# A 4-byte-per-partition transfer from a constant tile to the output, issued ahead of the first load of an RMSNorm-SiLU kernel

## The chip, the cores and the metric

The kernel runs on one core of one Trainium2 chip. The metric is the device time of one launch in microseconds (us); lower is better. A profiled execution gives, beside its time, a span: from the first to the last instruction in the trace. Five engines work side by side, each with its own instruction queue: TensorE (PE), VectorE (DVE), ScalarE (ACT), GpSimd (POOL) and SyncE (SP). Data moves between the memory (HBM, called DRAM in the code) and the on-chip SBUF by 16 DMA engines that all queues share. Here ScalarE and SyncE issue transfers; each has a DMA queue of its own (q10 for ScalarE's transfers, q1 for SyncE's).

## The reference

```python
x: (8, 1024, 2048) float32; gamma: (2048,) float32; eps = 1e-5
rms = np.sqrt(np.mean(x ** 2, axis=-1, keepdims=True) + eps)
out = gamma * x / rms
return out * (1 / (1 + np.exp(-out)))
```

Each of the 8192 rows of 2048 values is divided by its root mean square, multiplied by gamma, and put through SiLU. All of x is read once and all of the output written once, 67.1 MB each.

## The kernel before

**Tiling.** The 8192 rows are cut into 16 blocks (`nblk`) of 512 rows. A block is one SBUF tile `xt` of 128 partitions x 8192 values: partition p holds J = 4 whole rows, which lie side by side in memory, so each partition's part is one run of 32 KB. `xb[b]` and `ob[b]` are the views of input and output for block b. A pool of BUFS = 6 such tiles is used in turn; the work is done in place, so a block's tile is loaded, computed on and stored from, and can be loaded again only when its store has landed.

**Work on one block.** `squares_scalar` (L65) sums the squares of one or two of the four rows on ScalarE, `squares_vector` (L73) those of the others on VectorE. `root` (L82) takes the root on ScalarE, `invert` (L87) its reciprocal on VectorE. `multiply` (L92) is four VectorE instructions, one for each row: x times the reciprocal times gamma. `silu` (L98) is two ScalarE instructions of two rows each, and `store` (L102) sends the block out. The last block is done otherwise: `multiply` by gamma alone (L152) while the root is computed, then Silu with the reciprocal as its scale (L154).

**Order.** The order is written out by hand: the body stands in `tc.manual_schedule()`, so each engine's instructions run in the order of the program, and semaphores for the dependences are added by the framework, for writes to the output in memory as well. The first thing is six loads, issued by ScalarE one behind the other (L54). Then VectorE fills `ones` and `eps_t`, ScalarE runs a Square on one element (L110), and SyncE issues the load of gamma into one partition (L111). TensorE spreads gamma over 128 partitions (L114) and VectorE copies it into `g` (L115). Then the loop over blocks starts. Loads 6 to 15 are issued by ScalarE from within `squares_scalar`, three blocks ahead, each behind a wait for the store that frees its tile. All 16 stores are issued by SyncE, in order, each when its block's Silu is done.

**Queues.** ScalarE's queue holds both compute and load issues: an issue that waits holds up the compute behind it. SyncE's queue holds gamma's load and the 16 stores. A transfer signals its landing on one of eight semaphores that are taken in rotation.

**Constant tiles.** The framework's start-up has GpSimd fill small constant tiles before the kernel's body begins, among them one of 128 x 1 float32 zeros (`const-float32-0.0`).

Of the kernel before, what the change touches and what calls it, by code (L numbers as in the profile page):

```python
# [1 line left out]

# [4 lines left out]

ACT = mybir.ActivationFunctionType
ALU = mybir.AluOpType


@with_exitstack
def kernel(
    ctx: ExitStack,
    tc: tile.TileContext,
    x: bass.AP,
    gamma: bass.AP,
    eps: bass.AP,
    out: bass.AP,
):  # L20

    nc = tc.nc
    P = nc.NUM_PARTITIONS
    f32 = mybir.dt.float32
    x2 = x.flatten_outer_dims()
    o2 = out.flatten_outer_dims()  # L30
    n, d = x2.shape
    J = 4
    BUFS = 6
    nblk = n // (P * J)
    xb = x2.rearrange("(b p j) d -> b p (j d)", p=P, j=J)
    ob = o2.rearrange("(b p j) d -> b p (j d)", p=P, j=J)

    singles = ctx.enter_context(tc.tile_pool(name="singles", bufs=1))
    pool = ctx.enter_context(tc.tile_pool(name="pool", bufs=BUFS))
    small = ctx.enter_context(tc.tile_pool(name="small", bufs=2))  # L40
    psum = ctx.enter_context(tc.tile_pool(name="psum", bufs=1, space=bass.MemoryType.PSUM))

    Q = 4
    w = d // Q
    g = singles.tile([P, d], f32)
    eps_t = singles.tile([P, 1], f32)
    ones = singles.tile([P, P], f32)
    junk_a = psum.tile([P, d], f32, name="junk_a")
    junk_v = psum.tile([P, d], f32, name="junk_v")
    blocks, sss, rmss, rstds = {}, {}, {}, {}  # L50

    def load(b):
        xt = pool.tile([P, J * d], f32, name="xt")
        nc.scalar.dma_start(out=xt, in_=xb[b])  # L54
        blocks[b] = xt

    def row(b, j):
        return blocks[b][:, j * d:(j + 1) * d]

    def squares_scalar(b, loads=()):  # L60


        sss[b] = small.tile([P, J], f32, name="ss")
        for j in range(share(b)):
            nc.scalar.activation(out=junk_a, in_=row(b, j), func=ACT.Square,  # L65
                                 accum_out=sss[b][:, j:j + 1])
            if j == 0:
                for s in loads:
                    load(s)

    def squares_vector(b):
        for j in range(share(b), J):
            nc.vector.tensor_tensor_reduce(  # L73
                out=junk_v, in0=row(b, j), in1=row(b, j), scale=1.0, scalar=0.0,
                op0=ALU.mult, op1=ALU.add, accum_out=sss[b][:, j:j + 1])

    def share(b):
        return 1 if 4 <= b <= 12 and b % 2 == 0 else 2

    def root(b):  # L80
        rms = small.tile([P, J], f32, name="rms")
        nc.scalar.activation(out=rms, in_=sss.pop(b), func=ACT.Sqrt, scale=1.0 / d, bias=eps_t)  # L82
        rmss[b] = rms

    def invert(b):
        rstd = small.tile([P, J], f32, name="rstd")
        nc.vector.reciprocal(out=rstd, in_=rmss.pop(b))  # L87
        rstds[b] = rstd

    def multiply(b):  # L90
        for j in range(J):
            nc.vector.scalar_tensor_tensor(out=row(b, j), in0=row(b, j), scalar=rstds[b][:, j:j + 1],  # L92
                                           in1=g, op0=ALU.mult, op1=ALU.mult)

    def silu(b):
        for h in range(0, J, 2):
            cols = slice(h * d, (h + 2) * d)
            nc.scalar.activation(out=blocks[b][:, cols], in_=blocks[b][:, cols], func=ACT.Silu)  # L98
        store(b)

    def store(b):
        nc.sync.dma_start(out=ob[b], in_=blocks[b])  # L102

    with tc.manual_schedule():

        for b in range(BUFS):
            load(b)
        nc.vector.memset(ones, 1.0)  # L108
        nc.vector.memset(eps_t, float(eps))
        nc.scalar.activation(out=junk_a[:, 0:1], in_=ones[:, 0:1], func=ACT.Square)  # L110
        nc.sync.dma_start(out=g[0:1, :], in_=bass.AP(tensor=gamma.tensor, offset=gamma.offset, ap=[[d, 1], [1, d]]))  # L111
        for c in range(Q):
            cols = slice(c * w, (c + 1) * w)
            nc.tensor.matmul(junk_v[:, cols], ones[0:1, :], g[0:1, cols], start=True, stop=True)  # L114
        nc.vector.tensor_copy(out=g, in_=junk_v)  # L115

        last = nblk - 1
        SOON = 3  # L120
        squares_scalar(0)
        squares_vector(0)
        root(0)
        invert(0)
        for b in range(last):
            loads = [b + 3] if BUFS <= b + 3 < nblk else []
            if b < SOON:
                multiply(b)
                squares_scalar(b + 1, loads)
                silu(b)  # L130
                squares_vector(b + 1)
                root(b + 1)
            elif b < last - 1:
                squares_scalar(b + 1, loads)
                squares_vector(b + 1)
                root(b + 1)
                multiply(b)
                silu(b)
            else:
                multiply(b)  # L140
                squares_scalar(b + 1)
                silu(b)
                squares_vector(b + 1)
                root(b + 1)
            if b + 1 < last:
                invert(b + 1)


        for j in range(J):
            if j == J // 2:  # L150
                invert(last)
            nc.vector.tensor_mul(out=row(last, j), in0=row(last, j), in1=g)  # L152
        for j in range(J):
            nc.scalar.activation(out=row(last, j), in_=row(last, j), func=ACT.Silu,  # L154
                                 scale=rstds[last][:, j:j + 1])
        store(last)


# [1 line left out]
_INS = ['x', 'gamma', 'eps']  # L160
_OUTS = [((8, 1024, 2048), 'float32')]

_NUMBERS = {'eps': 9.999999747378752e-06}


# [26 lines left out]
```

## Time and profile before

| What | Value |
|---|---|
| median of five runs | 316.89 us |
| five runs, lowest to highest | 316.72 to 317.34 us |
| the profiled execution's own time | 316.89 us |
| its span | 315.1 us |
| busy: DVE, ACT, PE | 235.3, 213.9, 7.2 us |
| HBM read, written | 67.12 MB, 67.11 MB |
| share of the 16 DMA engines: q10 (loads), q1 (gamma and stores) | 49.7%, 49.4% |
| DMA packets; of these under 512 B | 4612; 513 |
| issue to landing, median: a load, a store | 38.7 us, 29.6 us |
| shortest: a load, a store | 12.3 us, 13.4 us |
| first and last load issue | 0.7 us, 240.5 us |
| first and last store issue | 35.2 us, 300.9 us |

A load or a store is 4.19 MB in 128 runs of 32 KB, 8 of them for each DMA engine, and each DMA engine ends its part with a 4-byte write to the semaphore. Those writes are the packets under 512 B: 16 for each of 32 transfers and one for gamma's. In the start of the trace GpSimd fills the constants at 0.23 to 0.43 us, and the first issues on both queues stand at 0.72 us. ScalarE's first Square on a block begins at 13.10 us, when the first load has landed.

### The profile page before, as it was taken

To read this page: it belongs to the slowest core of one execution; us is meant where nothing else is said; L and a number is where in the kernel's file an instruction comes from. 1 tells how busy PE (TensorE), PEld (TensorE's weight loads), DVE (VectorE), ACT (ScalarE), POOL (GpSimd) and SP (SyncE) were. 2 spreads that over 40 slices of the span, in tenths; PEclk is the share of its full clock that TensorE was granted. 3 is DMA by queue.
4 is the path that set the end of the run, shared out by engine and by line. 5 is a ranking of instruction groups with operands and counts; after the bars stand their busy time and mean duration, and the time that the engine had idled before them with its cause. 6 is when DMAs were issued, how large, how long until landed. Compare 5 with 4: busy or idle time off the path is not lost.

```text
span 315.1 us, 437 instructions
## 1 busy us (share of the span) xinstructions
PE 7.2 (2%) x8; PEld 2.5 (1%) x8; DVE 235.3 (75%) x157; ACT 213.9 (68%) x136; POOL 0.2 (0%) x4
## 2 busy tenths in 40 slices
PE   6200000000000000000000000000000000000000
PEld 2000000000000000000000000000000000000000
DVE  0679597979995795957969489593996929999600
ACT  1349998972799268682687827877278768779910
POOL 0000000000000000000000000000000000000000
DMA  8999999999999999999999999999999999999996
GB/s 334 408 458 408 395 462 408 458 416 449 416 450 412 450 412 453 416 449 420 445 424 441 433 433 437 428 437 428 441 424 441 424 441 424 445 420 449 416 449 287
DMA packets 4612, 134.24 MB, mean 426 GB/s; under 512 B 513, under 2 KB 513, under 8 KB 513
## 3 DMA queue, kind: packets, MB, share of 16 engines
q10 hardware_dynamic: 2304, 67.11, 49.7%
q1 hardware_dynamic: 2306, 67.12, 49.4%
q14 instruction: 2, 0.02, 0.0%
HBM read 67.12 MB, written 67.11 MB: 426 GB/s over the span
## 4 chain that ended last, share of the span: by engine, by line
DMA 68%; DVE 14%; ACT 11%; issue 2%; ACTq 1%; DVEq 0%
DMA xt<-in_x_dram 68%; DVE xt L92 9%; DVE junk_v L73 5%; ACT xt L98 4%; ACT junk_a L65 3%; ACT xt L154 2%; ACT L82 1%; ACTq L187 1%; ACT L154 0%; ACT L98 0%; ACT rms L82 0%; DVE ss L73 0%; ACTq L54 0%; DVE rstd L87 0%; ACTq L82 0%
## 5 line engine op out<-in xcount | busy, mean ns | idle before, releaser
L92 DVE SCALAR_TENSOR_TENSOR xt<-xt,rstd,g 128x2048 f32<-128x2048 f32 x60 | 137.0, 2346 | 0.1
L98 ACT ACTIVATE xt<-xt 128x4096 f32<-128x4096 f32 x30 | 108.3, 3615 | 27.1 <-DVE xt L92 27.0
L73 DVE CUSTOM_DVE_ANT_0 junk_v<-xt 128x2048 f32<-128x2048 f32 x37 | 85.1, 2299 | 43.0 <-DMA xt<-in_x_dram 42.3
L65 ACT ACTIVATE junk_a<-xt 128x2048 f32<-128x2048 f32 x27 | 50.7, 1877 | 22.4 <-DMA xt<-in_x_dram 22.0
L82 ACT ACT_TABLE_LOAD x15 | 19.2, 1283 | 27.6 <-DVE ss L73 27.5
L98 ACT ACT_TABLE_LOAD x14 | 18.0, 1283 | 0.2
L87 DVE RECIPROCAL rstd<-rms 128x4 f32<-128x4 f32 x16 | 2.8, 173 | 8.3 <-ACT rms L82 8.3
L152 DVE TENSOR_TENSOR xt<-xt,g 128x2048 f32<-128x2048 f32 x4 | 8.9, 2279 | 0.0
L115 DVE COPY g<-junk_v 128x2048 f32<-128x2048 f32 x1 | 2.3, 2291 | 8.8 <-PE junk_v L114 8.8
L82 ACT ACTIVATE rms<-ss,eps_t 128x4 f32<-128x4 f32 x16 | 4.8, 297 | 5.7 <-DVE ss L73 5.5
L154 ACT ACTIVATE xt<-xt,rstd 128x2048 f32<-128x2048 f32 x4 | 7.7, 1990 | 0.0
L114 PE MATMUL junk_v<-g,ones 1*128 1x512 f32 x8 | 7.2, 1072 | 2.6 <-DMA g<-in_gamma_dram 2.6
L73 DVE DVE_READ_ACCUMULATOR2_ANT ss<- 128x1 f32 x37 | 5.2, 141 | 0.0
L65 ACT ACTIVATION_READ_ACCUMULATOR junk_a<-xt 128x1 f32 x27 | 5.0, 186 | 0.0
L110 ACT ACT_TABLE_LOAD x1 | 1.3, 1283 | 4.0 <-issue 4.0
L114 PEld LDWEIGHTS junk_v<-g,ones 1*128 1x128 f32 x8 | 2.5, 325 | 5.7 <-issue 5.7
L154 ACT ACT_TABLE_LOAD x1 | 1.3, 1283 | 0.0
L108 DVE MEMSET ones<- 128x128 f32 x1 | 0.2, 165 | 0.8 <-PEq L173 0.8
L110 ACT ACTIVATE junk_a<-ones 128x1 f32<-128x1 f32 x1 | 0.2, 174 | 0.0
L173 POOL MEMSET const-bfloat16-1.0<- 128x1 bf16 x1 | 0.1, 101 | 0.0
L173 POOL MEMSET const-uint8-127<- 128x1 uint8 x1 | 0.1, 101 | 0.0
L173 POOL MEMSET const-float32-0.0<- 128x1 f32 x1 | 0.1, 98 | 0.2 <-issue 0.2
(2 smaller groups left out, 0.2 us busy)
## 6 DMA issues: line engine op xcount, KB each, us to landing
xt<-in_x_dram ACTq DMA_DIRECT2D x16, 4096.0 KB, 38.7
out_dram<-xt SPq DMA_DIRECT2D x16, 4096.0 KB, 29.6
g<-in_gamma_dram SPq DMA_DIRECT2D x1, 8.0 KB
```

Of the source, the lines that this page charges most:

```text
L65: nc.scalar.activation(out=junk_a, in_=row(b, j), func=ACT.Square, accum_out=sss[b][:, j:j + 1])
L73: nc.vector.tensor_tensor_reduce(out=junk_v, in0=row(b, j), in1=row(b, j), scale=1.0, scalar=0.0, op0=ALU.mult, op1=ALU.add, accum_out=sss ...
L82: nc.scalar.activation(out=rms, in_=sss.pop(b), func=ACT.Sqrt, scale=1.0 / d, bias=eps_t)
L87: nc.vector.reciprocal(out=rstd, in_=rmss.pop(b))
L92: nc.vector.scalar_tensor_tensor(out=row(b, j), in0=row(b, j), scalar=rstds[b][:, j:j + 1], in1=g, op0=ALU.mult, op1=ALU.mult)
L98: nc.scalar.activation(out=blocks[b][:, cols], in_=blocks[b][:, cols], func=ACT.Silu)
L110: nc.scalar.activation(out=junk_a[:, 0:1], in_=ones[:, 0:1], func=ACT.Square)
L114: nc.tensor.matmul(junk_v[:, cols], ones[0:1, :], g[0:1, cols], start=True, stop=True)
L115: nc.vector.tensor_copy(out=g, in_=junk_v)
L152: nc.vector.tensor_mul(out=row(last, j), in0=row(last, j), in1=g)
L154: nc.scalar.activation(out=row(last, j), in_=row(last, j), func=ACT.Silu, scale=rstds[last][:, j:j + 1])
L187: with _tile.TileContext(nc) as tc:
```

## The change

ScalarE issues one more transfer, in front of the six loads: the 128 x 1 tile of zeros goes to the first element of each partition's run in block 0 of the output, 128 pieces of 4 bytes that lie 32 KB apart in memory. Store 0 writes the same places later, so the framework lets it wait until this transfer has landed; the output is the same. Nothing else is changed; the lines below move down by two.

```diff
     with tc.manual_schedule():
 
+        zero = nc.const_aps.tensor(0.0, [P, 1], f32)
+        nc.scalar.dma_start(out=ob[0][:, 0:1], in_=zero, allow_slow_non_contiguous=True)
         for b in range(BUFS):
             load(b)
         nc.vector.memset(ones, 1.0)
```

## The prediction

> **What bounds the kernel now.** I read the page's slices first, then the queues, the chain of waits, windows of the DMA rows at the start, at the first store and at the end, and last what the issuing queues wait for. The slices, from the page:
>
> ```profile
> DVE  0679597979995795957969489593996929999600
> ACT  1349998972799268682687827877278768779910
> DMA  8999999999999999999999999999999999999996
> GB/s 334 408 458 408 395 462 408 458 416 449 416 450 412 450 412 453 416 449 420 445 424 441 433 433 437 428 437 428 441 424 441 424 441 424 445 420 449 416 449 287
> ```
>
> No compute engine is full, but the 16 DMA engines are busy from the first slice to the last. The alternation of 408 and 458 is counting: pieces of 32 KB are booked whole where they start. In windows that hold whole rounds of pieces it is gone (columns: window, its length, the five engines, clock, DMA share, GB/s):
>
> ```profile
> 26.79:38.88 12.10, 0.00 (x0) 0.00 (x0) 8.80 (x7) 12.02 (x8) 0.00 (x0) 1.00 1.01 415
> 50.98:63.08 12.10, 0.00 (x0) 0.00 (x0) 10.48 (x6) 11.46 (x9) 0.00 (x0) 1.00 1.00 433
> ...
> 278.50:302.69 24.19, 0.00 (x0) 0.00 (x0) 17.90 (x11) 21.56 (x13) 0.00 (x0) 1.00 1.00 433
> 300.00:312.10 12.10, 0.00 (x0) 0.00 (x0) 0.00 (x0) 0.84 (x1) 0.00 (x0) 1.00 1.00 433
> ```
>
> The ceiling is 433 GB/s, 27.06 GB/s per engine, or 1.21 us for one 32 KB piece. All 134.22 MB at that rate take 310.0 us of the 315.1 us span. The last line matters: even after the last load, while the tail computes, the engines still work off earlier stores, so a delay anywhere in the DMA reaches the end whole. Only 5.1 us of the span is not transfer at full rate. Three views show where part of that lies. First the chain of waits, at its start:
>
> ```profile
> 0.66 0.06 issue
> 0.72 0.38 ACTq L54
> 1.11 0.03 issue
> 1.14 21.57 DMA xt<-in_x_dram
> ```
>
> ScalarE's first issue starts at 0.72 us and its second at 1.14, 0.42 later. Then the DMA rows of 1.5 to 3.1 us (the first load's first round of pieces) and of 37.2 to 38.7 us (the round in which the first store, issued at 35.23, joins):
>
> ```profile
> DMA packets 18, 0.53 MB, mean 333 GB/s; under 512 B 1, under 2 KB 1, under 8 KB 1
> q10 hardware_dynamic: 16, 0.52, 116.0%
> q1 hardware_dynamic: 2, 0.01, 2.1%
> ```
>
> ```profile
> DMA packets 16, 0.52 MB, mean 350 GB/s; under 512 B 0, under 2 KB 0, under 8 KB 0
> q10 hardware_dynamic: 16, 0.52, 118.9%
> ```
>
> The percentage is packet time over 16 engines and the window. One load piece per engine took 1.160 x 1.6 = 1.86 us at the start and 1.189 x 1.5 = 1.78 us where the first store joins, against 1.21 in steady state: two one-time stalls of 0.65 and 0.57 us. The second agrees with the dip to 415 GB/s above: (1 - 415/433) x 12.1 = 0.50 us. No other 24.19 us window up to 302.69 us is under 432 GB/s.
>
> **The change part by part.** *The added issue (L107).* It stands on ScalarE's queue in front of all six first loads. Nothing shows an issue of such small pieces; I price it as a load's, which has 128 pieces too: the first issue delays the second by 0.42 us, and the six together took 3.21 us, 0.54 each. I take 0.42 (the same place in the queue) and keep 0.54 as the upper end. Loads 1 to 5 move too, but only the first matters: the six are 25.2 MB, 58 us at 433 GB/s, queued within 4 us. Behind them on ScalarE stand the table load at 3.96 us and the one-element Square; ScalarE then sits idle 7.67 us until the first load lands (13.10), which hides them. Gamma goes on SyncE's queue and is not moved in time; it shares the engines, and its copy ends at 12.10, 7.7 us before its first use by L92 at 19.82.
>
> *The 128 pieces of 4 bytes.* Each of 16 engines gets 8 and a completion write. The trace has no 4-byte data piece. Below, the nearest row is the completion write, 4 bytes too, in the last window (312.7 to 315.1 us):
>
> ```profile
> DMA packets 16, 0.00 MB, mean 0 GB/s; under 512 B 16, under 2 KB 16, under 8 KB 16
> q1 hardware_dynamic: 16, 0.00, 0.4%
> ```
>
> That is 0.004 x 2.4 us x 16 / 16 = about 0.01 us each, so 9 of them are 0.09 us per engine. Above, the smallest data piece is gamma's 8 KB: q1's 2.1% of 16 x 1.6 us is 0.54 us, less the 0.01 of its completion, against 8192 B / 27.06 GB/s = 0.30 by size: 0.23 us of overhead. Eight such are 1.84 us, and with one completion 1.85. I take the lower price, since size is what the piece shares with it, but add one stall: twice in this trace the first use of something in the DMA (first load; first write to the output) cost 0.57 to 0.65 us, and the pieces are now the first of their queue and the first write. Their work is then 0.65 + 0.09 = 0.74 us, of which the 0.42 us until the first load's pieces arrive is already counted: 0.32 more.
>
> By the Trainium skill ("DMA: Bandwidth & Descriptors", Specifications) a transfer under 512 B makes the engine read, modify and write, and its section on latency and other measured facts gives about 0.8 us as the least round trip to HBM. That speaks against the change: were the round trip blocking once, the 0.74 would be an estimate of 0.89 by that page, and the total 0.15 higher; were it blocking eight times, 6.4 us. No row here shows a 4-byte write to the output, but the completion writes behind 4 MB stores show no pause: the store-only window above stays at 433 GB/s across one.
>
> *The wait of the first store.* It is on SyncE's queue, in front of all 16 stores, for the tiny transfer's landing. That store is issued at 35.23 us, when its Silu ends. The tiny transfer, issued at 0.72, would have to take over 34 us to be felt; the whole first load took 12.3. Cost zero, hidden by load 0's compute. If the cover were gone, every us late would delay store 0, the reuse of its buffer by load 6, and all stores behind it. The semaphores of later transfers shift by one place in their rotation of eight; each transfer waits for the same predecessors as before, so nothing else is added.
>
> *What may be given back.* The 0.57 us stall at the first store may be the price of the first write to the output, which the tiny transfer now pays in advance, or the price of a second queue joining a running one (SyncE's), which it can't pay, as it runs on ScalarE's. Bounds 0 and -0.57; I take 0, because the stall stands on the load's pieces while a new queue starts, and the tiny transfer leaves that as it is.
>
> Sum: 0.42 + 0.32 + 0 + 0 = +0.74 us on a profiled execution of 316.89 us (span 315.1 and 1.8 around it), which is also the median of the five runs: 317.63. Own range: low 0.42 + 0.09 - 0.09 hidden in the 0.42 = +0.42 (no stall), high 0.54 + 0.65 + 1.85 - 0.42 = +2.62.
>
> **The rivals.** *A, the first store's stall is taken over.* The tiny write pays for the first write of each engine and the dip near 37 us goes: 0.74 - 0.57 = +0.17, 317.06. For it: the stall occurs once, at the first write to the output, though stores and loads take turns for 240 us after it. Against: gamma's queue start, the other joining, fell into the first load's stall and can't tell the two apart.
>
> *B, faster.* The place is the first round of both queues. The tiny pieces pay every first-use cost while load 0 is still being issued: load 0's first round drops from 1.86 to 1.21 (-0.65), the first store's too (-0.57), and in front stand only the issue and pieces, 0.42 + 0.09 = 0.51: -0.71, 316.18. It decides once over 0.51 us of the two stalls, 1.22 together, is gone; with one gone it is A or nothing. For it: both stalls look alike. Against: the load's may simply be the time until the first bytes of x come back, which a write elsewhere doesn't shorten.
>
> *C, heavy pieces.* At gamma's overhead of 0.23 us each: 0.42 + (0.65 + 1.85 - 0.42) = +2.50, 319.4; half of that overhead gives +1.58, 318.5. For it: nothing in the trace shows a small data piece cheaper than 0.54 us. Against: that is one row, taken inside the start stall.
>
> **How the numbers follow.** The forecast (front delay paid, nothing given back) has 0.46, A 0.16, B 0.20, C 0.18. The time is the forecast's, 317.6. About 0.2% (0.63 us; limits 316.26 and 317.52) is what a measurement of this kernel can tell from no change, its five runs spreading over 0.62 us. The forecast sits 0.11 us above that limit, and 0.06 of its 0.46 I put below it; with A the middle has 0.22. Faster is B, 0.20; slower is 0.40 + 0.18 = 0.58. The range goes down to 316.1, which takes in B's own value, and up to 318.9, which leaves out the upper half of C: about 0.1 is left out on each side. The forecast alone runs from 317.3 (+0.42) to 318.3 (half of C's surcharge).
>
> **What would show it.** Some 144 more packets, all under 512 B. ScalarE's first load issue 0.42 to 0.54 us later, the first load's landing later by 0.7; the dip to 415 GB/s still there near 38 us, and 433 everywhere else. If the dip is gone, A or B; if load 0's first round takes 1.21 us, B; if the tiny packets' queue time exceeds 1 us per engine, C. The forecast is wrong if the last store's issue (300.87) moves by less than 0.4 or more than 1.5 us, or if any window past 40 us leaves 433 GB/s: that would be a mechanism I have not seen.

## The result and the profile after

| | before | after |
|---|---|---|
| median | 316.91 us (49 runs) | 317.45 us (29 runs) |
| ratio | | 1.0017, 95% interval 1.0012 to 1.0022 |
| profiled execution: span | 315.1 us | 315.6 us |

The change makes the kernel 0.54 us slower, 0.38 to 0.70 by the interval of the ratio. That is within the 0.2% (0.63 us) which the prediction had called no change, and inside its range; the forecast was 317.6. Of all timed runs in this document one, 329.51 us of the kernel that writes 4 KB in advance, was in a slow state and is left out of its comparison.

First the page of the kernel after: the added packets and the issues.

```profile
DMA packets 4756, 134.24 MB, mean 425 GB/s; under 512 B 657, under 2 KB 657, under 8 KB 657
...
q10 hardware_dynamic: 2448, 67.11, 49.7%
q1 hardware_dynamic: 2306, 67.12, 49.3%
...
out_dram<-const-float32-0.0 ACTq DMA_DIRECT2D x1, 0.5 KB, 1.9
```

There are 144 more packets, all under 512 B and all on ScalarE's queue: 128 pieces and 16 completion writes. The tiny transfer lands 1.9 us after its issue, 33 us before the first store needs it. The chain of waits of the kernel after, at its start:

```profile
0.72 0.39 ACTq L107
1.11 0.03 issue
1.14 0.46 ACTq L54
```

The tiny issue now stands at 0.72 us and load 0's at 1.14: the 0.42 us of the prediction. What the DMA engines do meanwhile is in the DMA row of 1.5 to 3.5 us, in 40 slots of 0.05 us (busy tenths above, GB/s below). Before:

```profile
DMA  0060999999990990090000000000000000000009
GB/s 0 0 164 0 1311 1311 655 1311 655 1311 655 655 0 655 1311 0 0 655 0 0 0 0 0 0 0 0 0 0 0 0 0 0 0 0 0 0 0 0 0 655
```

After:

```profile
DMA  0094420000000199990909090000900090000000
GB/s 0 0 166 4 3 1 0 0 0 0 0 0 0 1 1966 655 1966 1966 0 655 0 655 0 655 0 0 0 0 1311 0 0 0 655 0 0 0 0 0 0 0
```

A packet is booked in the slot where it starts; 164 GB/s is gamma's 8 KB, 655 one piece of 32 KB. Before, load 0's first pieces start in the slot at 1.70 us. After, the 4-byte pieces (4, 3 and 1 GB/s) stand at 1.60 to 1.80, then nothing starts until load 0's pieces in the slot at 2.20, 0.50 us later than before, but for nine 4-byte packets at 2.15, right behind the completion write of gamma (one engine's share). So load 0 does not wait for the pieces to be worked off: for the last 0.4 us the other engines stand empty, until the next transfer reaches them. From the issue of load 0 to its first piece it is 1.06 us (1.14 to 2.20), against 0.98 before (0.72 to 1.70): of the 0.50, 0.42 are the issue. How long a 4-byte piece takes is in the DMA row of 1.2 to 2.2 us of the kernel after:

```profile
DMA packets 145, 0.01 MB, mean 9 GB/s; under 512 B 144, under 2 KB 144, under 8 KB 144
q10 hardware_dynamic: 143, 0.00, 7.7%
```

0.077 x 16 x 1.0 us / 143 is 8.6 ns. Load 0's first round is as slow as it was: in the window of 1.5 to 3.5 us its 16 pieces and the tiny ones stand as

```profile
q10 hardware_dynamic: 160, 0.52, 95.0%
```

which is 1.90 us per engine, or 1.82 us without nine packets of 8.6 ns each, against 1.86 before. The last of the 16 pieces of this round starts in the slot at 3.10 us, before at 2.35, and the first load lands when the last engine is through. ScalarE's first Square begins 0.73 us later than before (13.10):

```profile
13.83 1.88 ACT L65 ACTIVATE junk_a<-xt 128x2048 f32<-128x2048 f32 x1 [7.94 <-DMA xt<-in_x_dram]
```

The first store's issue goes with it (35.98 instead of 35.23). The prediction gave 0.7 for that landing; the end moved by less.

The stall where the first store joins is still there (windows of whole rounds, columns as in the prediction):

```profile
27.20:39.30 12.10, 0.00 (x0) 0.00 (x0) 8.78 (x8) 12.04 (x9) 0.00 (x0) 1.00 1.00 417
37.10:61.29 24.19, 0.00 (x0) 0.00 (x0) 21.89 (x14) 22.39 (x17) 0.00 (x0) 1.00 1.00 419
61.29:85.48 24.19, 0.00 (x0) 0.00 (x0) 22.27 (x17) 13.29 (x10) 0.00 (x0) 1.00 1.00 433
```

417 and 419 GB/s around the first store, as 415 and 419 before, and 433 behind it. At the other end, the completion writes of the last store: before, 9 of the 16 DMA engines write theirs between 313.0 and 313.3 us; after, 10 of them between 313.6 and 313.9. The delay of the start has gone through 310 us of saturated DMA and comes out at the end.

### The profile page after: what moved, and what is told of

The parts are those of the page before. It is cut to its first block, busy times and chain, and to the rows that moved or that the text cites. A ratio compares the mean times of both kernels' runs of the same rounds, so it can differ in the third digit from the quotient of the medians.

```text
span 315.6 us, 438 instructions
## 1 busy us (share of the span) xinstructions
PE 7.2 (2%) x8; PEld 2.5 (1%) x8; DVE 235.3 (75%) x157; ACT 213.7 (68%) x136; POOL 0.2 (0%) x4
## 4 chain that ended last, share of the span: by engine, by line
DMA 68%; DVE 14%; ACT 11%; issue 2%; ACTq 1%; DVEq 0%
DMA xt<-in_x_dram 68%; DVE xt L92 9%; DVE junk_v L73 5%; ACT xt L98 4%; ACT junk_a L65 3%; ACT xt L156 2%; ACT L82 1%; ACTq L189 1%; ACT L156 0%; ACT L98 0%; ACT rms L82 0%; DVE ss L73 0%; ACTq L54 0%; ACTq L107 0%; DVE rstd L87 0%
```

## The experiments

The theory after the first result: the change costs the place of one transfer in front of load 0, that is, the 0.5 us by which load 0's pieces start later, and its size, its direction and the wait of the first store cost nothing. The rivals: the 4-byte pieces or the write to HBM cost it (a cold start, slow pieces); or the first store's wait does. Each kernel was timed against the kernel before on the same chip. The diffs of the first seven stand against the changed kernel, the others against the kernel before.

**Behind load 0 instead of in front of it.**

```diff
         for b in range(BUFS):
             load(b)
+            if b == 0:
+                nc.scalar.dma_start(out=ob[0][:, 0:1], in_=zero, allow_slow_non_contiguous=True)
```

(and the line in front of the loop is gone)

> The tiny transfer is issued by ScalarE behind load 0 instead of in front of it; its pieces and the first store's wait stay. If the 0.54 us that the change costs is the place in front of load 0 (0.42 us of issue, 0.6 us until load 0's pieces start), it falls to the pieces alone, 9 x 0.01 = 0.09 us: 317.0. If it is the pieces (a cold start, a slow 4-byte write) or the store's wait, it stays near 317.45, wherever the transfer stands.

317.20 against 316.94 us, ratio 1.0007 (0.9998 to 1.0016): not told apart from no change, though the interval (up to 0.51 us) also overlaps the change's. Load 0's pieces start in the slot at 1.70 us again. By itself this run leans to the place as the cost; the next one, which is clearer, decides. (The 1.6 us that this expectation and the next name as the start of the pieces is gamma's slot; load 0's is 1.70.)

**Issued by SyncE.**

```diff
-        nc.scalar.dma_start(out=ob[0][:, 0:1], in_=zero, allow_slow_non_contiguous=True)
+        nc.sync.dma_start(out=ob[0][:, 0:1], in_=zero, allow_slow_non_contiguous=True)
```

> The tiny transfer is issued by SyncE in front of gamma, so ScalarE's first load issue is back at 0.72 us. If the cost is ScalarE's issue slot: 317.0, load 0's pieces at 1.6 us as before. If both queues' transfers are prepared one after another by something shared, load 0 starts up to 0.5 us later: 317.2 to 317.4. If the stall of 0.57 us at the first store (37 us) is the price of the first write on SyncE's queue, the dip to 415 GB/s goes, and the time falls to 316.4 to 316.9; if it is the price of two busy queues meeting, the dip stays.

317.02 against 316.94 us, ratio 0.9999 (0.9989 to 1.0009): no cost that shows. The same 128 pieces to the same place, with the same wait of the first store, are free when they don't stand in ScalarE's queue. The DMA row of this kernel, 1.5 to 3.5 us:

```profile
DMA  0055399909990009000900000000000000000000
GB/s 0 0 4 4 2 656 1966 2621 0 1311 655 1966 0 0 0 655 0 0 0 655 0 0 0 0 0 0 0 0 0 0 0 0 0 0 0 0 0 0 0 0
```

Here the pieces of both queues follow each other with no empty slot: the pieces at 1.60 to 1.75, load 0's from 1.75. So a transfer on the other queue does not hold load 0 up, and one on the same queue does. What was held up is gamma, now second on SyncE's queue: TensorE's first matmul, which waits for it, began at 7.15 us instead of 2.61, and the first store was issued at 36.16 instead of 35.23. The time did not follow that, so a later first store alone is not what the change costs. The stall at the first store did not go (one round of 16 load pieces between 38.4 and 39.9 us takes 115.1% of 1.5 us, 1.73 us each, and 33.0 to 45.1 us runs at 412 GB/s), so a first small write on SyncE's queue doesn't pay for it.

**Two in front.**

```diff
         nc.scalar.dma_start(out=ob[0][:, 0:1], in_=zero, allow_slow_non_contiguous=True)
+        nc.scalar.dma_start(out=ob[0][:, 1:2], in_=zero, allow_slow_non_contiguous=True)
```

> Two such transfers in front of load 0, on the first and the second column. If each costs its issue slot: 0.54 more, or 0.46 to 0.6, so 317.9 to 318.1, and load 0's issue at about 1.6 us. If the cost is paid once (a cold start of the queue or of the first write): near 317.55.

318.27 against 316.94 us, ratio 1.0039 (1.0026 to 1.0052): +1.33 us by the medians, more than twice the change. Load 0's issue is at 1.62 us as expected, but its pieces start only in the slot at 2.90, 1.20 later than before. By the medians the time follows the pieces (1.20) rather than the issue (0.90), but its interval, 0.82 to 1.65 us, takes in both. From the issue of load 0 to its first piece it is now 1.28 us, where it was 0.98 with none and 1.06 with one such transfer in front. That the queue prepares its transfers one behind the other, and more slowly than ScalarE issues them, would fit this; no row shows the preparing itself.

**One piece instead of 128.**

```diff
-        nc.scalar.dma_start(out=ob[0][:, 0:1], in_=zero, allow_slow_non_contiguous=True)
+        nc.scalar.dma_start(out=ob[0][0:1, 0:1], in_=zero[0:1, :], allow_slow_non_contiguous=True)
```

> The tiny transfer has one piece of 4 bytes (partition 0 alone) instead of 128, still in front of load 0. If the cost is that of issuing a transfer whatever its pieces: 317.4. If it goes by pieces (their preparation or their work on the engines): 1/128 of it, so 316.9 to 317.1, with load 0's issue less than 0.2 us later.

317.61 against 316.94 us, ratio 1.0019 (1.0011 to 1.0028): the cost of the change, with one 4-byte piece. It is the transfer, not its pieces. ScalarE is even held longer (its next issue stands at 1.28 us instead of 1.14), and load 0's pieces start in the slot at 2.25, 0.97 us behind the issue as in the kernel before. Here the issue alone makes the delay: it is 0.56 us later, the pieces 0.55.

**64 times the pieces.**

```diff
-        zero = nc.const_aps.tensor(0.0, [P, 1], f32)
-        nc.scalar.dma_start(out=ob[0][:, 0:1], in_=zero, allow_slow_non_contiguous=True)
+        zero = nc.const_aps.tensor(0.0, [P, 64], f32)
+        nc.scalar.dma_start(out=ob[0][:, 0:128:2], in_=zero, allow_slow_non_contiguous=True)
```

> Same place in front of load 0, but 64 pieces of 4 bytes per partition (every second element of the first 128), 8192 in all, 512 per DMA engine. One look at the price of a piece. If a piece costs its row in the trace, 0.01 us: 512 x 0.01 = 5 us of engine time ahead of load 0, 322. If the pieces are written at gamma's overhead of 0.23 us each: about 118 us more. If the preparation of the transfer goes by its pieces, ScalarE's next issue comes later than 0.42 us as well.

365.57 against 316.88 us, ratio 1.153 (1.152 to 1.155): +48.7 us for 512 pieces per DMA engine, 95 ns each if all of it is put down to them, eleven times their price in the change and under half of gamma's 0.23. Two stretches of this kernel's DMA rows show both prices, first 1.0 to 3.1 us, then 5 to 10 us:

```profile
DMA packets 1650, 0.01 MB, mean 7 GB/s; under 512 B 1649, under 2 KB 1649, under 8 KB 1649
```

```profile
DMA packets 973, 0.00 MB, mean 1 GB/s; under 512 B 973, under 2 KB 973, under 8 KB 973
```

In the first, 1648 pieces start within about 1 us, over 100 per engine; in the second 973 in 5 us, 61 per engine, 82 ns each. The first hundred and more per engine are taken at once, those behind them at about an eighth of that rate. With 8 per engine the change stays on the cheap side. This transfer also holds ScalarE's queue: the six loads behind it take 33.20 us to issue.

**A tiny load instead of a tiny store.**

```diff
-        zero = nc.const_aps.tensor(0.0, [P, 1], f32)
-        nc.scalar.dma_start(out=ob[0][:, 0:1], in_=zero, allow_slow_non_contiguous=True)
+        probe = singles.tile([P, 1], f32, name="probe")
+        nc.scalar.dma_start(out=probe, in_=xb[0][:, 0:1], allow_slow_non_contiguous=True)
```

> In place of the tiny store, a tiny load: 128 pieces of 4 bytes from block 0 of x into an SBUF tile that nothing reads, same place on ScalarE's queue; no store waits for a write to the output. If the cost is the place of an issue in front of load 0: 317.4 to 317.6, as with the change. If the write to HBM or the store's wait carries part of the 0.54 us, it is less. If a first touch of x shortens load 0's first round (1.86 us), less too, down to 316.9.

317.47 against 316.88 us, ratio 1.0017 (1.0008 to 1.0026): the same cost without a write to the output. Load 0's pieces start in the slot at 2.20. A first touch of x gains nothing.

**Into the last block, so that the first store doesn't wait.**

```diff
-        nc.scalar.dma_start(out=ob[0][:, 0:1], in_=zero, allow_slow_non_contiguous=True)
+        nc.scalar.dma_start(out=ob[nblk - 1][:, 0:1], in_=zero, allow_slow_non_contiguous=True)
```

> The tiny store goes to block 15 of the output, so the first store no longer waits for it (the last one does, 300 us later). If the first store's wait costs nothing: 317.45, as the change. If it carries the cost: 316.9.

317.49 against 316.88 us, ratio 1.0021 (1.0012 to 1.0030): the same cost without the first store's wait. The wait is free.

**The same delay without any transfer.**

```diff
+        nc.vector.memset(ones, 1.0)
+        nc.scalar.activation(out=junk_a[:, 0:1], in_=ones[:, 0:1], func=ACT.Square)
         for b in range(BUFS):
             load(b)
-        nc.vector.memset(ones, 1.0)
...
-        nc.scalar.activation(out=junk_a[:, 0:1], in_=ones[:, 0:1], func=ACT.Square)
```

> No tiny transfer; ScalarE's table load and one-element Square (1.28 and 0.17 us in the trace before) go in front of load 0 instead of behind load 5. No DMA is added. If the end follows the start of load 0 one to one, whatever stands in front of it: 1.5 us later, 318.4 (318.2 to 318.6), with load 0's issue near 2.2 us. If the start has slack, or the cost of the change is in the DMA and not in ScalarE's queue: 316.9 to 317.3.

317.24 against 316.85 us, ratio 1.0012 (1.0003 to 1.0021): slower, but by 0.39 us, not by 1.5. By its number alone this is the rival's case (316.9 to 317.3). The timeline of this kernel says why it is not (start, duration, engine):

```profile
0.72 1.28 ACT L107 ACT_TABLE_LOAD   x1 [0.72 <-PEq L173]
...
1.03 1.34 ACTq L54 DMA_DIRECT2D xt<-in_x_dram  x3
2.02 0.17 ACT L107 ACTIVATE junk_a<-ones 128x1 f32<-128x1 f32 x1
```

The first load is issued at 1.03 us, while the table load in front of it still runs to 2.00 and the Square has not begun. The load is only 0.31 us late; that fits the Square's wait for the tile of ones, which VectorE has filled at 1.00 us. Load 0's pieces start in the slot at 2.00, 0.30 later than before, and the end comes 0.39 later (0.10 to 0.67 by the interval). So a delay of the first load's start reaches the end without any transfer in front of it.

Taken together, the start of load 0's pieces (slots of 0.05 us) and the time against the kernel before of the same comparison (difference of medians):

| kernel | load 0's pieces, slot | later by | time, later by |
|---|---|---|---|
| before | 1.70 | | |
| issued by SyncE | 1.75 | 0.05 | 0.08 |
| behind load 0 | 1.70 | 0.00 | 0.26 |
| Square first, no transfer | 2.00 | 0.30 | 0.39 |
| the change | 2.20 | 0.50 | 0.54 |
| tiny load | 2.20 | 0.50 | 0.59 |
| into the last block | 2.20 | 0.50 | 0.61 |
| one piece | 2.25 | 0.55 | 0.67 |
| two in front | 2.90 | 1.20 | 1.33 |

The intervals of these differences are about 0.15 to 0.4 us to each side, so the table shows that the time follows the start about one to one, not tenths.

**Loads on both queues from the start** (against the kernel before), a try at the stall of 0.57 us:

```diff
-        nc.scalar.dma_start(out=xt, in_=xb[b])
+        eng = nc.sync if b in (1, 3, 5) else nc.scalar
+        eng.dma_start(out=xt, in_=xb[b])
```

(gamma's load is issued in front of the loop of loads)

> Another start, without the tiny transfer: loads 1, 3 and 5 are issued by SyncE behind gamma, the others by ScalarE. Theory: the stall of 0.57 us where the first store joins is that of two queues meeting, so with both busy from the start it falls into the start and is gone: 316.3 to 316.5. Rival: load 0 now shares the engines with load 1 and lands some 9 us later, and the stores stand behind loads 3 and 5 on SyncE's queue; if the DMA runs dry for that, slower, up to some 9 us: 317 to 326.

317.20 against 316.88 us, ratio 1.0011 (1.0003 to 1.0020): no gain. Windows of this kernel:

```profile
32.00:44.10 12.10, 0.00 (x0) 0.00 (x0) 10.33 (x8) 10.43 (x6) 0.00 (x0) 1.00 1.00 433
56.20:68.30 12.10, 0.00 (x0) 0.00 (x0) 10.36 (x8) 11.03 (x9) 0.00 (x0) 1.00 0.97 395
68.30:80.40 12.10, 0.00 (x0) 0.00 (x0) 10.30 (x10) 6.44 (x5) 0.00 (x0) 1.00 1.00 433
```

SyncE's first 32 KB pieces start only behind 6.0 us, but from there both queues are busy, and the stretch around 38 us is at full rate; the dip has moved to where the first store (issued at 39.86) gets its turn, behind load 5 on SyncE's queue. The last round of load pieces there, between 59 and 60 us, takes 184.0% of 1.0 us, 1.84 us each, and between 57 and 60 us ScalarE's queue moves no data. So it isn't the price of a second queue joining. It goes with the store.

**A larger write in advance** (against the kernel before), the tile of ones with 512 bytes per partition:

```diff
+        nc.sync.dma_start(out=ob[0][:, 0:P], in_=ones)
         nc.sync.dma_start(out=g[0:1, :], in_=bass.AP(tensor=gamma.tensor, offset=gamma.offset, ap=[[d, 1], [1, d]]))
```

> Without the tiny transfer; SyncE writes 128 pieces of 512 bytes to block 0 of the output in front of gamma (a store that store 0 overwrites). If the stall of 0.57 us at the first store belongs to the first write of more than a few bytes and can be paid in advance in the shadow of ScalarE's first issue: the dip near 37 us goes, 316.3 to 316.6. If it belongs to the first stores following loads on busy engines: it stays, and 128 x 512 bytes cost 0.15 us: 316.9 to 317.2.

The second kernel writes 4 KB per partition from a tile of its own.

> The same with 128 pieces of 4 KB, 8 per DMA engine, 1.2 us at full rate. If a write of real size pays the stall in advance: the dip goes, and 1.2 - 0.57 = +0.6 us, 317.5. If not: +1.2 us, 318.1, less what of it runs before load 0's pieces start.

319.69 (median of six runs) and 319.14 to 322.18 (five runs, three at 319.2 and two at 322) against 316.97 us, ratios 1.0082 (1.0065 to 1.0099) and 1.0114 (1.0081 to 1.0148): both miss, for a reason that neither theory named. The timeline of the kernel with 512 bytes:

```profile
17.06 7.16 PE L115 MATMUL junk_v<-g,ones 1*128 1x512 f32 x8 [17.06 <-DMA g<-in_gamma_dram]
```

Gamma's load stands behind the early write on SyncE's queue, and that write only started once ScalarE's loads were running: its landing took 13.5 us. Gamma came at 17.06 instead of 2.61 us, and the first store was issued at 46.06 instead of 35.23 (with 4 KB: gamma at 19.16, the store at 48.16). Where the 2.7 us of the kernel with 512 bytes come from is shown only in part: its windows behind 133 us are at 432 to 433 GB/s up to 302.6 us, but its engines end unevenly, with three 32 KB pieces still starting between 313 and 315 us, where the kernel before has none. As for the stall, 395 and 401 GB/s from 48.2 to 60.3 us show it still there in both kernels, now where the late first store joins. In the kernel with 4 KB it comes a second time: from 98.3 to 106 us SyncE's queue has no data to move and only loads run, and the window of 96.60 to 108.70 us, in which the store issued at 102.21 starts, is at 406 GB/s, 0.75 us short of 433. So it is not tied to the first store alone; it fits a store that starts after a stretch of loads alone, seen once more here and not tested. No version tried beats the kernel before.

## Why the prediction was right or wrong

**The bound: right.** The DMA engines, busy throughout, passed a delay of their start on to the end about one to one. The table above shows it over 0 to 1.3 us, and the Square in front shows it without a transfer.

**The issue, 0.42 us: right in the trace, short as a price.** Load 0 is issued 0.42 us later, its pieces start 0.50 later, and two transfers make 1.20 of 0.90 us of issue. The price of a place in front of load 0 is 0.5 to 0.6 us. The end kept as the upper one, 0.54 from six issues in a row, came out nearer; that it equals the measured 0.54 is luck, as the interval is 0.38 to 0.70.

**The 4-byte pieces, 0.09 us: right in size, wrong in place.** About 0.01 us each was read from the completion writes, and 8.6 ns were measured for 8 per engine. But they lie within the 0.5 us until load 0's pieces arrive: one piece in place of 128 cost no less.

**The cold start of 0.65 us, 0.32 of it exposed: wrong.** This is the step that failed. The pieces show no first-use stall: they are through at about 1.8 us and the engines stand empty behind them, and no pause of 0.8 us, once or for each of the eight, shows either. The stall stayed on load 0's first round (1.82 us per engine), from which it had been carried over. Of the 0.32 exposed, 0.08 are left by the trace (0.50 less the issue's 0.42) and 0.12 by the time. Without that step the sum is +0.42 to +0.54, and the measured +0.54 is its upper end; with it the forecast came out 0.2 us too high and on the wrong side of the 0.2% line. The sign that did come out, the first load landing 0.73 later, is luck for this step: it hangs on the one engine that begins its first piece last, it was 0.50, 0.48 and 0.73 later with one piece, the tiny load and the last block, and the time does not go with it (0.67, 0.59 and 0.61).

**The first store's wait, zero: right** (the kernel that writes to the last block).

**What may be given back, zero: right, for a reason that doesn't hold.** The stall stayed, but not because a queue joins: with loads on both queues from the start it moved with the first store. Nor was it paid in advance by writes of 4 bytes, 512 bytes or 4 KB per partition. Rivals A and B fall with it; B's sign, a first round of 1.21 us, did not come. Rival C falls at 8 pieces per engine; heavy pieces were seen only in the run of 512, at 95 ns instead of 230.

**One of the tests that the prediction set itself was badly chosen.** The last store's issue was to move by 0.4 to 1.5 us, or the forecast was wrong; it moved from 300.87 to 300.97, so by this test it was. But the test doesn't go with the time: the issue moved by 0.67, 0.73 and 0.60 us with one piece, the tiny load and the last block, at the cost of the change, and by -1.46 on SyncE, at none. It hangs on the last load's landing (279.16 to 279.27), and that on the DMA engine that is furthest behind. In the kernel before one load of the chain took 39.25 us instead of 38.67 (104.48 to 143.73). In that stretch the DMA row holds an 8 KB packet of the instruction queue, which takes one engine 0.3 us:

```profile
q14 instruction: 1, 0.01, 1.3%
```

(window of 108.0 to 109.5 us of the kernel before; 0.013 x 16 x 1.5 us.) The same packet is fetched in the kernel after, where the chain shows no such step. That may be why the last landing lost most of the start's delay; that the packet hit the engine that was last was not shown. The end, set by all engines working off the stores, was late by the whole delay (span 315.6 against 315.1 us).

## What to carry to other kernels

Where the DMA engines are busy from the first transfer to the last, as here, what a small transfer costs is the start it takes from the first large one: here 0.5 to 0.6 us for each transfer in front of it on the same queue, whether it has 1 piece or 128 (8192 pieces cost 48.7), and nothing that shows on the other queue. So put small transfers on a queue that doesn't carry the first large load, but not in front of something that the compute needs early; behind the first load on its own queue the cost was 0.26 us, told apart neither from none nor from the whole. And price them by when the next transfer's pieces start, not by their bytes.

## What was not expected of the hardware

- The price of a 4-byte write has two regimes: 8.6 ns for 8 per DMA engine, 82 to 95 ns in a run of 512, with the change after more than a hundred.
- A transfer of one piece held ScalarE's queue longer than one of 128 (0.52 against 0.39 us).
- An issue in ScalarE's queue did not wait for the activation in front of it to run: a load was issued at 1.03 us while the table load ahead of it ran until 2.00.
- The first store costs the DMA engines a stall (0.57 us in the kernel before) that moves with that store, and that no earlier write tried here pays. It came once more, with 0.75 us, when a later store started after some 8 us of loads alone. Its cause stays open.
